# A two-layer decoder trunk on one core: casts set behind Pool's sums, zeros stored later, the join of the attention groups on Pool, fewer dense shares per strided item

## Chip, cores and metric

One core of one Trainium2 chip. The metric is device time in microseconds (us) of one execution; three runs of the kernel before gave 2818.04, 2818.78 and 2820.15, median 2818.78. Engines: PE = TensorE (matmuls), DVE = VectorE, ACT = ScalarE, POOL = GpSimd, SP = SyncE, which here issues all DMAs in one order. Each engine runs its instructions in the order of its own list.

## The reference, cut to what matters

Two layers over 1024 tokens of width 1024, in float32. Each layer adds to x the output of two attentions that run side by side, then that of a gated feed-forward part with a causal convolution.

```python
h = rmsnorm(x, norm1[l])
proj = h @ w_in[l]          # 1024 x 5120: q, k, v of both mixers, and the gates
o_a = dilated_mixture(qa, ka, va)        # 3 groups of 4 heads: dilation 1, 4, 16
o_b = stick_breaking_attention(qb, kb, vb)   # 4 heads
g_a, g_b = split(sigmoid(gate_pre + b_gate[l]))
x = x + (g_a * (o_a @ w_br[l, :256]) + g_b * (o_b @ w_br[l, 256:])) @ w_o[l]
h2 = rmsnorm(x, norm2[l])
a, v = split(h2 @ w_up[l])
x = x + (gelu(conv(a)) * v) @ w_down[l]
```

In the dilated mixture each group of heads does a softmax over a window of every 1st, 4th or 16th key, and the outputs of the three groups are added with weights proportional to their softmax denominators. The last step is a final RMSNorm.

## The kernel before

Every float32 operand of a large product is split into a high part (a cast to a rounded type on ACT, line 123) and a low part (source minus high part, on DVE, line 124); three matmuls of the parts make one product. Activations lie with features on the 128 partitions and tokens along the free axis, in two halves of 512 tokens. Part of the dense products are made with seven block products in place of eight (`pair`, `seven`): their operands are sums and differences of blocks of the weights (made in `pair`, lines 915 to 925) and of h (made in `block_sums`, lines 862 to 892: for the first two of four series Pool does three operations per sum, lines 871 to 873, into a buffer h_sum, and `split` casts it into t_hi and t_lo).

A layer's first part is a sequence of attention items, with dense products woven in. The items are 16 of the stick-breaking mixer (names B00 to B17), four of the group with dilation 1 (N00 to N11: scores z and lines 679 and 680, transposes t at line 688, parts p0h and p0l, products o at line 700), and 16 of the strided groups with dilation 4 and 16 (T00 to T17: scores z<-t_kq at lines 571 and 572, lines 780 and 781, transposes t at lines 786 to 788, parts p1h and p1l, products o at lines 796 and 798). Each item is cut into steps. After each step `Dense.advance(rate)` adds the item's rate to an account, and for every whole unit PE gets one share of dense work, six matmuls of 128x512 in `pair`. `RATE` holds the rates: stick-breaking, dilation 1, and the strided items of the first and of the second pair of heads. What dense work is left after the last item is done in `finish`. `Dense.aside`, called once per step, takes the next piece of side work from a list as soon as the item that it names is done; the 16 sums of h are that list. A strided item may begin when its keys and queries, fetched into t_kq, have had six shares of time. PE's order is the program's order; a scheduler orders the other engines and SP from estimated times.

`join(pr)` (lines 809 to 839) puts the groups together for a pair of heads, after the last strided item of that pair: small DVE steps on 128x16 tiles make the weights (lines 818 to 827), a DMA writes them to df, four DMAs bring them back broadcast over the partitions as fn and ft (line 833), and four DVE operations make `on` = `on` x fn + ot x ft (lines 834 to 839). After the second join, `in_two` in `mixer` casts `on` into oh_a and ol_a, and the branch product br_ps (lines 149 to 151) reads them, first for the first pair of heads and then for the second.

In layer 0, `mixer` also fills `none` with zeros on Pool (line 1069) and stores it four times into tk (line 1073), since the low part of the queries fills only half of its rows. `first` loads x in eight pieces xr and normalizes them with gb, a broadcast of the gains held in the buffer with the tag "ot".

Of the kernel before, what the change touches and what calls it, by code (L numbers as in the profile page):

```python
# [6 lines left out]
F32 = mybir.dt.float32  # L7
# [4 lines left out]
ALU = mybir.AluOpType  # L12
# [3 lines left out]
P = 128  # L16
# [21 lines left out]
IN_ORDER = {ET.PE, ET.Activation, ET.DVE, ET.Pool}  # L38
HEAD = 4
SECOND = 0.35  # L40
RATE = (0.68, 0.85, 1.0, 0.85)
PLAIN = 8
LEAD = 6
AHEAD = 200
# [2 lines left out]
def f32(ap):  # L47
    return ap.bitcast(F32)
# [3 lines left out]
def trunk_kernel(ctx, tc, x, norm1, w_in, b_gate, w_br, w_o, norm2, w_up, conv_w, conv_b, w_down, norm_f, out, depth=None, probe=None):  # L52
    nc = tc.nc
    act, dve, pe, pool = nc.scalar, nc.vector, nc.tensor, nc.gpsimd
# [4 lines left out]
    sb = ctx.enter_context(tc.tile_pool(name="sb", bufs=1))  # L59
# [45 lines left out]
    tk = [dr.tile([2, 4, P, 6, 256], F32, name=f"tk{i}") for i in range(2)]  # L105
# [16 lines left out]
    def split(hi, lo, src):  # L122
        act.copy(hi, src)  # L123
        dve.tensor_tensor(lo, src, f32(hi), ALU.subtract)  # L124
# [292 lines left out]
    S, B = {}, {}  # L417
# [392 lines left out]
    def join(pr):  # L810

        st, on, ot = R["st1", pr], R["on"], R["ot", pr]
        sn = sb.tile([P, 2, 2, 2, 4], F32, tag="sn", bufs=1, name="sn")
        nc.sync.dma_start(sn.rearrange("j a s n r -> j (a s) n r"), tok_view(dn[pr]))
        nat, far_ = (t.rearrange("j a s n r -> j a (s n r)") for t in (sn, st))
        w = sb.tile([P, 6, 16], F32, tag="sw", bufs=1, name="sw")
        f = sb.tile([P, 2, 16], F32, tag="sf", bufs=1, name="sf")
        dve.tensor_tensor(w[:, 0, :], nat[:, 0, :], far_[:, 0, :], ALU.min)
        dve.tensor_tensor(w[:, 1, :], w[:, 0, :], nat[:, 0, :], ALU.subtract)
        dve.tensor_tensor(w[:, 2, :], w[:, 0, :], far_[:, 0, :], ALU.subtract)  # L820
        act.activation(w[:, 1:3, :], w[:, 1:3, :], AF.Exp)
        dve.tensor_tensor(w[:, 3, :], w[:, 1, :], nat[:, 1, :], ALU.mult)
        dve.tensor_tensor(w[:, 4, :], w[:, 2, :], far_[:, 1, :], ALU.mult)
        dve.tensor_tensor(w[:, 3, :], w[:, 3, :], w[:, 4, :], ALU.add)
        dve.reciprocal(w[:, 5, :], w[:, 3, :])
        dve.tensor_tensor(f[:, 0, :], w[:, 1, :], w[:, 5, :], ALU.mult)
        dve.tensor_tensor(f[:, 1, :], w[:, 2, :], w[:, 5, :], ALU.mult)
        nc.sync.dma_start(tok_view(df[pr]), f.rearrange("j a (s n r) -> j (a s) n r", s=2, n=2))
        fn = sb.tile([P, T], F32, tag="p4", bufs=4, name="fn")
        ft = sb.tile([P, T], F32, tag="p4", bufs=4, name="ft")  # L830
        for a, t in enumerate((fn, ft)):
            for s in range(2):
                nc.sync.dma_start(t[64 * s : 64 * s + 64, :], df[pr][2 * a + s, :].partition_broadcast(64))
        dve.tensor_tensor(on[:, pr, :], on[:, pr, :], fn, ALU.mult)
        for n in range(2):
            src = ot.rearrange("p (r n j) -> p n j r", r=4, n=2)[:, n]
            fv = ft.rearrange("p (n j r) -> p n j r", n=2, r=4)[:, n]
            dve.tensor_tensor(fv, src, fv, ALU.mult)
        dve.tensor_tensor(on[:, pr, :], on[:, pr, :], ft, ALU.add)


    def half(n, k):
# [17 lines left out]
    def block_sums():  # L860


        keep = {}

        def first(t, a, b, i):
            if i == 0:
                if "r" not in keep:
                    keep["r"] = quarter("h_sum")
                new_s(t)
            r, (ah, al), (bh, bl) = keep["r"][:, i, :], a()[i], b()[i]  # L870
            pool.tensor_tensor(r, f32(al), f32(bl), ALU.subtract)
            pool.tensor_tensor(r, r, f32(ah), ALU.add)
            pool.tensor_tensor(r, r, f32(bh), ALU.subtract)
            split(*S[t][i], r)

        def further(t, a, i):
            if t == 4:

                S[4] = half(0, 0)
            elif i == 0:  # L880
                new_s(t)
            r, (ah, al) = keep["r"][:, i, :], a()[i]
            dve.tensor_tensor(r, f32(ah), r, ALU.subtract)
            dve.tensor_tensor(r, r, f32(al), ALU.add)
            split(*S[t][i], r)

        b11, b12, b21, b22 = (lambda n=n, k=k: half(n, k) for k in range(2) for n in (1, 0))
        todo = [({"B17"}, lambda i=i: first(3, b22, b12, i)) for i in range(4)]
        todo += [({"N01s"}, lambda i=i: first(1, b12, b11, i)) for i in range(4)]
        todo += [({"N11s"}, lambda i=i: further(2, b22, i)) for i in range(4)]  # L890
        todo += [({"plain"}, lambda i=i: further(4, b21, i)) for i in range(4)]
        return todo

    def pair(dense, l, offs, tiled, put):

# [168 lines left out]
    def mixer(l, pending):  # L1064
        R.clear()
        if l == 0:
            masks()
            none = sb.tile([P, 8, 256], F32, tag="xa", bufs=4, name="none")
            pool.memset(none[0:64], 0.0)
            for pr in range(2):  # L1070
                for g in range(2):
                    there = tk[pr][:, :, 64:128, 3 * g + 2, :].rearrange("s r p c -> p (s r) c")
                    nc.sync.dma_start(there, none[0:64])
        vectors = setup(l)
        next(vectors)
        first_units = relay(heads.pop(l)[0], primed=True) if l else relay(head(l))
# [3 lines left out]
        dense = Dense()  # L1080
        dense.plain = [gate(l, c) for c in range(PLAIN)]
        dense.seven = [pair_gate(dense, l, e) for e in range(PLAIN // 2, KD)]
        dense.side = block_sums()

        def kq(name, pr, after, off, scale):
            offk, offq = (OFF_KB, OFF_QB) if name == "b" else (OFF_KA, OFF_QA)
# [16 lines left out]
        for pr in range(2):  # L1103
            for i in range(8):
                needs = ["b1"] if pr else []
                items.append((f"B{pr}{i}", needs, [], RATE[0], lambda pr=pr, i=i: stick_item(pr, i // 4, i % 4)))
        for pr in range(2):
            for s in range(2):
                items.append((f"N{pr}{s}", [f"0{pr}"], ["v0"], RATE[1], lambda pr=pr, s=s: near_item(pr, s)))
        for pr in range(2):  # L1110
            share = {}
            for i in range(8):
                if i % 4 == 0:
                    share = {}
                items.append((f"T{pr}{i}", [f"F{8 * pr + i}"], [], RATE[2 + pr], lambda pr=pr, i=i, share=share: far_item(dense, pr, i // 4, i % 4, share)))
        attend(dense, items)
# [7 lines left out]
        def in_two():  # L1124
            for nm, src in (("b", R["ob"]), ("a", R["on"])):
                hi, lo = big("oh_" + nm, F32R), big("ol_" + nm, F32R)
                for n in range(2):
                    for c in range(2):
                        sl = slice(n * HF, (n + 1) * HF)
                        split(hi[:, c, sl], lo[:, c, sl], src[:, c, sl])  # L1130
                oh[nm] = (hi, lo)

        branches()
        todo = [(n, e0 + i) for e0 in range(0, KD, 2) for n in range(2) for i in range(2)]
# [567 lines left out]
    def first():  # L1702
        gb = sb.tile([P, T], F32, tag="ot", name="gb")
        warm = sb.tile([P, 8], F32, tag="ss", bufs=2, name="warm")
        act.activation(warm[:, 0:1], eps, AF.Sqrt)
        wp = bank("t", "warm")
        for _ in range(WARM):
            pe.matmul(wp[:, 0:P], ident, ident, start=True, stop=True)
        for n in range(2):
            new_h(n)  # L1710
            for c in range(4):
                t0 = n * HF + c * P
                xr = sb.tile([P, T], F32, tag="p4", bufs=4, name="xr")
                nc.sync.dma_start(xr, xin[t0 : t0 + P, :])
                if n == 0 and c == 0:
                    nc.sync.dma_start(gb, norm1[0].partition_broadcast(P))
                sq = sb.tile([P, T], F32, tag="ql", bufs=2, name="xsq")
                ss = sb.tile([P, 8], F32, tag="ss", bufs=2, name="ss")
                act.activation(sq, xr, AF.Square, accum_out=ss[:, 0:1])
                act.activation(ss[:, 1:2], ss[:, 0:1], AF.Sqrt, bias=eps[:, 0:1], scale=1.0 / D)  # L1720
                dve.reciprocal(ss[:, 2:3], ss[:, 1:2])
                for e0 in (0, 4):
                    hd = slice(e0 * P, (e0 + 4) * P)
                    dve.scalar_tensor_tensor(xr[:, hd], xr[:, hd], ss[:, 2:3], gb[:, hd], ALU.mult, ALU.mult)
                    tp = bank("s", "x_t")
                    for e in range(4):
                        pe.transpose(tp[:, e * P : (e + 1) * P], xr[:, (e0 + e) * P : (e0 + e + 1) * P], ident)
                    tv = tp.rearrange("p (e t) -> p e t", e=4)
                    hi, lo = (h[:, e0 : e0 + 4, c * P : (c + 1) * P] for h in H[n])
                    split(hi, lo, tv)  # L1730
                yield
# [46 lines left out]
```

## Time and profile before

| what | value |
|---|---|
| median of three runs | 2818.78 us |
| the profiled execution | 2819.48 us |
| its span from first to last instruction | 2817.7 us |
| mean granted PE clock | 0.983 |
| busy PE, DVE, ACT, POOL | 2692.9, 2001.3, 1354.3, 658.4 us |
| layer 0, layer 1: first score of a strided item | 444.1, 1833.2 us |
| the same: br_ps that waits for oh_a starts | 613.3, 2004.2 us |

The profile page has, for the whole span: busy time per engine; the span in 40 slices; DMA queues; the chain that ended last; the costliest groups of instructions. Further views give the waits (which engine and line waited for whom: total us, times, longest), busy time in chosen windows (length; busy us and instructions of PE, of PE's weight loads, of DVE, ACT and POOL; granted PE clock; DMA share; GB/s), and the instructions in order of time. Matmuls are pipelined, so one that takes 0.39 us follows its neighbour by about 0.23 us.

### The profile page before, as it was taken

How to read it: one execution, taken by the hardware profiler on the slowest of the kernel's cores; microseconds unless marked ns; L12 is line 12 of the kernel's file. 1: busy time of each engine (PE TensorE's matmuls, PEld its weight loads, DVE VectorE, ACT ScalarE, POOL GpSimd, SP SyncE). 2: the span in 40 equal slices, each digit the busy share in tenths (PEclk: the TensorE clock that was granted, in tenths of full speed). 3: DMA queues.
4: the chain of work that ended last, by engine and by line, in shares of the span. 5: the costliest groups of instructions: out<-in, count | busy, mean ns of one | idle time of the engine just before them, and what ended most of it. 6: DMA issues, size and time to landing. Idle time of an engine off the chain costs nothing. (4 is left out here: it accounts for less than half of the span.)

```text
span 2817.7 us, 36591 instructions
## 1 busy us (share of the span) xinstructions
PE 2692.9 (96%) x13066; PEld 2247.1 (80%) x13066; DVE 2001.3 (71%) x2968; ACT 1354.3 (48%) x2494; POOL 658.4 (23%) x469
## 2 busy tenths in 40 slices
PE   8998999989999999999999989999799999999999
PEld 7877888868878888878888778888588787877888
DVE  5775656666678888887657755465658788888865
ACT  4655545455445455422345555454545455544225
POOL 1004111102234343431120041210122433433200
PEclk9999999989999999999999999999899999999999
DMA  4011258654334434588401122775732444446963
GB/s 140 27 49 59 78 155 260 189 192 159 88 120 140 159 129 148 196 326 294 177 33 36 42 72 83 202 232 173 238 102 79 132 137 165 142 157 223 332 244 120
DMA packets 362242, 424.77 MB, mean 151 GB/s; under 512 B 25180, under 2 KB 289740, under 8 KB 360524
## 3 DMA queue, kind: packets, MB, share of 16 engines
q1 hardware_dynamic: 362060, 422.44, 45.6%
q8 instruction: 103, 1.69, 0.3%
q14 instruction: 79, 0.65, 0.1%
HBM read 282.78 MB, written 139.59 MB: 150 GB/s over the span
## 5 line engine op out<-in xcount | busy, mean ns | idle before, releaser
L124 DVE TENSOR_TENSOR w_lo<-up_a,w_hi 128x512 fp32r<-128x512 f32 x240 | 231.7, 966 | 37.9 <-ACT w_hi L123 37.9
L123 ACT CAST w_hi<-up_a 128x512 fp32r<-128x512 f32 x240 | 149.4, 623 | 173.2 <-PE u_b L855 38.5
L1534 DVE TENSOR_TENSOR x<-x,d_ps 128x512 f32<-128x512 f32 (+1 forms) x228 | 152.4, 672 | 80.9 <-PE d_ps L1528 80.0
L1271 POOL TENSOR_TENSOR cv<-cv 128x512 f32<-128x512 f32 x88 | 125.4, 1435 | 266.3 <-DVE g L124 130.2
L124 DVE TENSOR_TENSOR g<-cv,g 128x512 fp32r<-128x512 f32 x154 | 168.0, 1101 | 0.1
L124 DVE TENSOR_TENSOR w_lo<-w_raw,w_hi 128x512 fp32r<-128x512 f32 x152 | 113.6, 753 | 67.2 <-ACT w_hi L123 63.5
L123 ACT CAST w_hi<-w_raw 128x512 fp32r<-128x512 f32 x152 | 93.9, 620 | 120.1 <-PE o_ps L150 66.5
L854 PE MATMUL u_a<-hh,w_hi 128*128 128x512 f32 x320 | 127.6, 399 | 19.0 <-ACT g L123 14.3
L123 ACT CAST w_hi<-in_a 128x512 fp32r<-128x512 f32 x120 | 74.5, 620 | 146.9 <-PE i_a L855 61.0
L124 DVE TENSOR_TENSOR w_lo<-in_a,w_hi 128x512 fp32r<-128x512 f32 x120 | 87.8, 732 | 80.3 <-ACT w_hi L123 80.1
L1526 PE MATMUL d_ps<-gd_in,w_hi 128*128 128x512 f32 (+1 forms) x340 | 130.7, 384 | 5.8 <-ACT g L123 5.8
L1527 PE MATMUL d_ps<-gd_in,w_hi 128*128 128x512 f32 (+1 forms) x340 | 130.6, 384 | 0.0
L1528 PE MATMUL d_ps<-gd_in,w_lo 128*128 128x512 f32 (+1 forms) x340 | 130.5, 384 | 0.0
L856 PE MATMUL u_a<-hh,w_lo 128*128 128x512 f32 x320 | 126.3, 395 | 4.2 <-DVE w_lo L124 4.2
L123 ACT CAST g<-cv 128x512 fp32r<-128x512 f32 x154 | 93.5, 620 | 76.3 <-DVE g L124 41.0
L855 PE MATMUL u_a<-hl,w_hi 128*128 128x512 f32 x320 | 126.2, 394 | 0.0
L854 PE MATMUL u_a<-t_hi,w_hi 128*128 128x512 f32 x320 | 124.7, 390 | 0.4 <-ACT u L1407 0.4
L856 PE MATMUL u_a<-t_hi,w_lo 128*128 128x512 f32 x320 | 124.6, 390 | 0.0
L855 PE MATMUL u_a<-t_lo,w_hi 128*128 128x512 f32 x320 | 124.6, 390 | 0.0
L614 DVE TENSOR_TENSOR_SCAN stay<-stay,zero 128x128 f32<-128x128 f32 (+3 forms) x64 | 86.9, 1357 | 38.7 <-ACT stay L612 38.5
L1526 PE MATMUL d_ps<-gd_in,wd 128*128 128x512 f32 (+1 forms) x292 | 114.0, 390 | 0.0
L1528 PE MATMUL d_ps<-gd_in,wd 128*128 128x512 f32 (+1 forms) x292 | 112.9, 387 | 0.0
(397 smaller groups left out, 8630.5 us busy)
## 6 DMA issues: line engine op xcount, KB each, us to landing
gd<-g SPq DMA_DIRECT2D x154, 512.0 KB, 3.4
gd_in<-gd SPq DMA_DIRECT2D x154, 512.0 KB, 6.1
up_a<-in_w_up_dram SPq DMA_DIRECT2D x80, 512.0 KB, 4.5
t_kq<-tk SPq DMA_DIRECT2D x32, 768.0 KB, 5.1
wd_raw<-in_w_down_dram SPq DMA_DIRECT2D x22, 1024.0 KB, 6.9
w_raw<-in_w_in_dram SPq DMA_DIRECT2D x80, 256.0 KB, 3.0
in_a<-in_w_in_dram SPq DMA_DIRECT2D x40, 512.0 KB, 5.4
gin<-gs SPq DMA_DIRECT2D x32, 512.0 KB, 4.3
```

The costliest lines, as they stand in the source:

```text
L123: act.copy(hi, src)
L124: dve.tensor_tensor(lo, src, f32(hi), ALU.subtract)
L614: dve.tensor_tensor_scan(rev, rev, zero[:, 0:1].to_broadcast([P, L]), 1.0, ALU.mult, ALU.add)
L854: pe.matmul(o, w[0][:, c], rh, start=(first and i == 0), stop=False, skip_group_check=True)
L855: pe.matmul(o, w[0][:, c], rl, start=False, stop=False, skip_group_check=True)
L856: pe.matmul(o, w[1][:, c], rh, start=False, stop=(last and i == 3), skip_group_check=True)
L1271: return lambda: pool.tensor_tensor(dst, a, dst, ALU.subtract)
L1526: pe.matmul(o[:, sub], wh[:, c], gh[:, sub], start=(i == 0 and k in (0, 4, 5)), stop=False, skip_group_check=True)
L1527: pe.matmul(o[:, sub], wh[:, c], gl[:, sub], start=False, stop=False, skip_group_check=True)
L1528: pe.matmul(o[:, sub], wl[:, c], gh[:, sub], start=False, stop=(i == m - 1), skip_group_check=True)
L1534: dve.tensor_tensor(x, x, o[:, sub], ALU.add)
```

## The change

There are four edits. `RATE` for the strided items falls from 1.0 and 0.85 to 0.72 and 0.62. The four operations at the end of `join` move from DVE to Pool. In `block_sums` the sum and its split become two pieces of side work: in the two series that Pool computes, the sums are begun every third step and each split follows four steps after its sum; in the two that DVE computes, the split follows one step later. The zeros are no longer filled and stored at the start, but as a piece of side work after item B02, from a buffer of half the size (in "ot") with eight stores instead of four.

```diff
-RATE = (0.68, 0.85, 1.0, 0.85)
+RATE = (0.68, 0.85, 0.72, 0.62)
...
-        dve.tensor_tensor(on[:, pr, :], on[:, pr, :], fn, ALU.mult)
+        pool.tensor_tensor(on[:, pr, :], on[:, pr, :], fn, ALU.mult)
...
-            dve.tensor_tensor(fv, src, fv, ALU.mult)
-        dve.tensor_tensor(on[:, pr, :], on[:, pr, :], ft, ALU.add)
+            pool.tensor_tensor(fv, src, fv, ALU.mult)
+        pool.tensor_tensor(on[:, pr, :], on[:, pr, :], ft, ALU.add)
...
             pool.tensor_tensor(r, r, f32(bh), ALU.subtract)
-            split(*S[t][i], r)
...
             dve.tensor_tensor(r, r, f32(al), ALU.add)
-            split(*S[t][i], r)
+
+        def in_two(t, i):
+            split(*S[t][i], keep["r"][:, i, :])
...
-        todo = [({"B17"}, lambda i=i: first(3, b22, b12, i)) for i in range(4)]
-        todo += [({"N01s"}, lambda i=i: first(1, b12, b11, i)) for i in range(4)]
-        todo += [({"N11s"}, lambda i=i: further(2, b22, i)) for i in range(4)]
-        todo += [({"plain"}, lambda i=i: further(4, b21, i)) for i in range(4)]
+        todo = []
+
+        def series(after, t, f, lag, gap):
+
+            at = {}
+            for i in range(4):
+                at.setdefault(i * gap, []).append(lambda i=i: f(i))
+                at.setdefault(i * gap + lag, []).append(lambda i=i: in_two(t, i))
+            for k in range(3 * gap + lag + 1):
+                todo.append((after, lambda fs=at.get(k, ()): [g() for g in fs]))
+
+        series({"B17"}, 3, lambda i: first(3, b22, b12, i), 4, 3)
+        series({"N01s"}, 1, lambda i: first(1, b12, b11, i), 4, 3)
+        series({"N11s"}, 2, lambda i: further(2, b22, i), 1, 1)
+        series({"plain"}, 4, lambda i: further(4, b21, i), 1, 1)
         return todo
+
+    def zeros():
+
+        none = sb.tile([P, 4, 256], F32, tag="ot", name="none")
+        pool.memset(none[0:64], 0.0)
+        for pr in range(2):
+            for g in range(2):
+                for s in range(2):
+                    nc.sync.dma_start(tk[pr][s, :, 64:128, 3 * g + 2, :].rearrange("r p c -> p r c"), none[0:64])
...
-            none = sb.tile([P, 8, 256], F32, tag="xa", bufs=4, name="none")
-            pool.memset(none[0:64], 0.0)
-            for pr in range(2):
-                for g in range(2):
-                    there = tk[pr][:, :, 64:128, 3 * g + 2, :].rearrange("s r p c -> p (s r) c")
-                    nc.sync.dma_start(there, none[0:64])
...
-        dense.side = block_sums()
+        dense.side = [({"B02"}, zeros)] * (l == 0) + block_sums()
```

## Prediction, on record before the changed kernel's time was known

> **What bounds the kernel now.** I read part 1 of the page first, then the waits of TensorE (PE), then the granted clock in windows around the longest of them, then the timeline there.
>
> ```profile
> PE 2692.9 (96%) x13066; PEld 2247.1 (80%) x13066; DVE 2001.3 (71%) x2968; ACT 1354.3 (48%) x2494; POOL 658.4 (23%) x469
> ```
>
> PE is the bound, and the change neither adds nor removes a matmul. Only its 2817.7 - 2692.9 = 124.8 us of idle time, and matmuls that ran at half clock, can be won. The waits of PE name whom it waited for (total us, times, longest):
>
> ```profile
> PE br_ps L149 <- ACT oh_a L123: 19.7, 2, 11.2
> PE o L700 <- ACT p0h L123: 18.5, 4, 6.4
> ...
> PE sb_t L625 <- DVE beta L615: 12.5, 10, 2.4
> PE z L571 <- DVE st L780: 8.5, 6, 2.1
> ...
> PE v_ps L149 <- ACT w_hi L123: 4.7, 1, 4.7
> ```
>
> Four of these lie where the change works: the join of the groups (oh_a), the casts around the sums of h (p0h), the scores during the first join (z), the start (v_ps). The windows show the second price, the seventh figure (PEclk) falling to 0.50 after idle:
>
> ```profile
> 258.70:269.00 10.30, 6.21 (x18) 5.05 (x19) 5.56 (x11) 5.57 (x16) 10.30 (x9) 0.50 0.31 120
> ...
> 279.20:282.60 3.40, 3.40 (x11) 2.71 (x11) 3.40 (x9) 2.70 (x7) 0.00 (x0) 0.50 0.44 128
> ...
> 535.20:542.00 6.80, 5.44 (x18) 4.57 (x19) 4.62 (x9) 4.19 (x11) 0.73 (x1) 0.50 0.35 117
> 589.80:593.20 3.40, 2.32 (x16) 2.03 (x17) 1.96 (x7) 1.39 (x4) 0.00 (x0) 1.00 0.51 131
> 593.20:596.60 3.40, 3.39 (x14) 2.71 (x14) 2.21 (x9) 2.79 (x9) 0.00 (x0) 0.50 0.65 275
> ```
>
> A half-clock window costs half of PE's busy time in it: 3.1 us in the first.
>
> **1. Start (layer 0 only).** SP issues four 512 KB stores of zeros at 7.2 us, ahead of the third and fourth w_raw loads; these land at 22.3 and 23.0, and PE idles 4.67 us until 23.0. In the changed order the fourth xr and the two w_raw stand there, behind only the DVE splits of the first two w_raw, which ended at 9.9 and 11.6; with some 4 us to landing the weights are there by 16, while PE has work until 18.3. The gap goes, and the 3.2 us after it at 0.21 us per matmul (0.12 from 26.3 on) shrink to about half. I take 6 us; the ends are 0 (another load binds) and 8. The zeros, now eight stores of 256 KB, stand behind the last xr and wait for the last reader of gb, since they share its buffer; SP had nothing to issue from 31.6 to 51.2, and 2 MB at 150 to 250 GB/s take 8 to 14 us, so they hide there. Without that cover the next w_raw would be up to 10 us late.
>
> **2. Casts of the sums.** The timeline shows the chain (start, length, last what ended the idle time):
>
> ```profile
> 254.75 1.73 POOL L871 TENSOR_TENSOR h_sum<-hl 128x512 f32<-128x512 f32 x1
> ...
> 255.26 1.77 DVE L124 TENSOR_TENSOR w_lo<-w_raw,w_hi 128x512 fp32r<-128x512 f32 x1
> ...
> 260.62 0.62 ACT L123 CAST t_hi<-h_sum 128x512 fp32r<-128x512 f32 x1 [5.88 <-POOL h_sum L873]
> ...
> 262.65 0.58 PE L700 MATMUL o<-p0h,v 128*128 128x256 f32 x1 [6.42 <-ACT p0h L123]
> ```
>
> ACT is in order: the cast of the third sum waits 5.88 us for Pool, the cast of p0h stands behind it, and PE waits. Layer 0 pays 6.42 + 2.91 + 0.62 idle and 3.1 + 1.7 at half clock, 14.7 us; layer 1 (1648 to 1683) 14.6. In the changed order p0h stands ahead, and the four casts of the first series stand together after the copies of the second half of the keys. Counted in shares (six matmuls at 0.227, 1.36 us) ACT gets there at about 261.7, when the twelve Pool operations from 245.1 are done (261.8). The next p0h is then ready at 265.5, just when PE wants it, its low part at 266.1. The second series starts on Pool when the first cast has freed h_sum (264), takes 12 x 1.28 = 15.4 us, and ends at 279.5 to 280.5; PE wants the p0h behind it at 281.9. So nothing long is left, but two places with no margin: I leave 1.4 us of stalls per layer and take 13.2 x 2 = 26.4 us. Ends: 18 (each place costs 2 us and a half-clock window) and 29.
>
> **3. The strided stage and its end.** From the first z<-t_kq to the br_ps that waits for oh_a took 444.1 to 613.3 = 169.2 us, in layer 1 1833.2 to 2004.2 = 171.0. The instruction orders hold 75 dense shares there before and after. Two items with twelve shares took 21.65 us (446.4 to 468.1), so an item's own work is (21.65 - 12 x 1.36) / 2 = 2.65 and PE's work is 16 x 2.65 + 75 x 1.36 = 144.4 us. The rest is waiting and half clock. Before, no share was left for the last two items; now ten shares and four pairs of transposes and products, 16.6 us, stand after the last score.
>
> What ends last is the chain of the join:
>
> ```profile
> 606.83 1.22 DVE L834 TENSOR_TENSOR on<-on,fn 128x1024 f32<-128x1024 f32 x1 [2.28 <-DMA fn<-df]
> ...
> 609.35 1.98 DVE L838 TENSOR_TENSOR ft<-ot,ft 128x512 f32<-128x512 f32 x2 [1.30 <-DMA ft<-df]
> ...
> 611.37 1.22 DVE L839 TENSOR_TENSOR on<-on,ft 128x1024 f32<-128x1024 f32 x1
> ...
> 612.63 1.14 ACT L123 CAST oh_a<-on 128x512 fp32r<-128x512 f32 x2 [1.55 <-DVE on L839]
> ```
>
> Scores (594.1), small DVE steps (to 598.4), df out and fn, ft back (609.3), three multiplies and adds, cast, PE: 19.2 us from last score to br_ps, 21.4 in layer 1. The change lengthens it twice. On Pool a 128x512 operation takes 1.28 (the h_sum rows), so 128x1024 some 2.5: after ft two of 1.28 and one of 2.5 stand for 1.98 + 1.22, +1.9 us (the multiply by fn hides between the landings of fn and ft). Strided Pool operations are in no row; the dearest simple one took 3.1 (L915), hence +0 to +5.5. And a w_lo that waits for PE to free a buffer (3.4 us after the last score) now stands before the last small steps: +2.6. The chain becomes 23.7 and 25.8 us.
>
> Then layer 0 needs 144.4 - 16.6 + 23.7 = 151.5 plus stalls s, layer 1 153.6 + s: they save 17.7 - s and 17.4 - s.
>
> s: fewer shares mean less time for DVE and ACT. Between a pair of transposes and the product that reads it lay 3.0 to 4.7 us; now about nine of 32 have 1.6. The chain needs 0.05 + 0.47 + 0.05 + 0.56 = 1.15, with one foreign cast (0.62) before it 1.75. I put 2.5 us on these, 0.9 on two scores that now stand together (as at 592.4), and 2.5 on the first join: Pool's 8 us of work meet DVE's splits, and the w_lo above took 1.77 against 0.69 alone because a Pool sum ran. Behind that split p1l and the scores wait. On the other side the DVE join at 529 to 537, which cost 3.4 us of idle and 2.7 at half clock, is gone. One half-clock window, 1.7, comes on top; rounded, s = 8, ends 3 and 14. So 9.5 per layer, 19 us; ends 7 and 29.
>
> The Trainium skill, page "SBUF — State Buffer", section "SBUF: two separate sides", says that Pool and a DVE operation with two SBUF inputs lock a shared port for the whole instruction, the other blocking. The trace agrees (1.77 against 0.69); by it a split beside the 2.5 us multiply can wait all of it, four such locks per first join.
>
> **Sum**, against the profiled execution's 2819.48 us (span 2817.7; the median of the runs, 2818.78, is 0.7 below): 2819.5 - 6 - 26.4 - 19 = **2768 us**.
>
> **Rivals.**
> (a) Short stalls bring no half clock, queues stay short, s = 3: 2768 - 10 = 2758. For it: twenty-odd gaps of 0.84 to 1.5 us had 1.00 after them. Against: the window 589.8 to 593.2, 2.32 of 3.40 busy, was followed by 0.50. The page "TensorE: Matmul & The Clock Gate" of the Trainium skill, section "What's actually happening", has the half rate come after an idle window of some 3.4 us, which would favour this rival; the trace differs, since that window held no such gap.
> (b) The end of the join eats its gain: strided Pool operations at 3.1, gate loads late behind the last stores: +5 to +8 per layer, 2768 + 13 = 2781.
> (c) The casts still wait: Pool's sums late by 3 us each and a half-clock window every time, 6 us per layer: 2780.
> (d) Slower: the thin cover makes the strided stage a chain of half-clock windows. A missed cover costs about 1.1 us and then 1.7; the 51 us are gone at 18 misses, 9 of 16 items in each layer. For it: 1.6 us of cover. Against: covers of 1.8 and 2.1 us at 540 to 580 showed no gap. At 24 misses: 2768 + 67 = 2835.
> (e) The orders move and nothing else, PE waits elsewhere: 2819.
>
> **Chances.** Forecast (2762 to 2775) 0.45; (a) 0.20; (b) 0.13; (c) 0.10; two of (b), (c) and a start without gain together, 2790 to 2800, 0.05; (d) 0.05; (e) 0.02. The range 2750 to 2796 leaves out (d), (e), and gains at every upper end. Faster by over 0.2% (about what a measurement of this kernel can tell from no change) 0.93, within 0.02, slower 0.05.
>
> **What would show it.** Right: v_ps without a 4.7 us gap before 25 us; no L700 wait over 1 us; the oh_a wait down from 8.5 and 11.2 to some 5 to 7 although its chain is longer; z waits under 1.5 us; a few L796 waits of 0.2 to 1 us. Wrong, if p0h still waits for the sums, if PEclk is below 0.9 in several slices of the strided stage, or if the keys' weights at 50 us come late behind the zeros.

## The result, and the profile after

The changed kernel takes 2775.99 us (median of four runs, 2774.71 to 2777.19). The kernel before, run beside it, takes 2819.47 (2818.04 to 2821.08). The ratio is 0.9846, 95% interval 0.9829 to 0.9863: faster by 1.5%. The forecast was 2768; 51.4 us were to be saved, 43.5 are (44.6 between the two profiled spans, 2817.7 and 2773.1).

Part 1 of the page of the changed kernel (busy us, share of the span, instructions):

```profile
PE 2679.4 (97%) x13066; PEld 2237.9 (81%) x13066; DVE 1989.5 (72%) x2952; ACT 1354.6 (49%) x2494; POOL 691.9 (25%) x485
```

PE has the same 13066 instructions. Its idle time fell from 124.8 to 93.7 us (span less busy), and its busy time by 13.5 us. Some 10 us of that are half clock: PE was busy for 58.8 us at half clock before and for 39.1 after, and half of such time is lost. DVE gave 16 instructions to Pool. The waits of PE in the changed kernel (total us, times, longest):

```profile
PE br_ps L149 <- ACT oh_a L123: 15.6, 2, 9.4
...
PE br_ps L149 <- ACT br_w L123: 7.8, 2, 6.7
...
PE o L700 <- DVE p0l L124: 4.5, 2, 2.3
...
PE o L796 <- DVE p1l L124: 3.6, 7, 0.8
...
PE z L571 <- DVE st L780: 1.4, 2, 0.7
...
PE o L700 <- ACT p0h L123: 0.5, 2, 0.3
```

The wait for p0h, 18.5 us before, is 0.5. The wait of the scores z is 1.4 for 8.5. The 4.7 us of v_ps at the start are gone. Two rows grew by over 2 us: p0l (1.2 us before) and br_w (5.3 us before in three waits, now with one of 6.7).

A table by stretches shows where the time went. Each is read from the starts of the named instructions on PE, in both profiled executions:

| stretch | before, layers 0 and 1 | after | saved | forecast |
|---|---|---|---|---|
| start to first score z of layer 0 | 77.1 | 69.0 | 8.1 | 6 |
| first score to first strided score | 367.0, 367.7 | 357.8, 358.1 | 18.7 | 26.4 |
| first strided score to the br_ps that waits for oh_a | 169.2, 170.9 | 156.4, 158.3 | 25.4 | 19 |
| from there to the first product u_ps | 141.6, 140.5 | 143.8, 144.6 | -6.3 | 0 |
| all the rest | | | -1.4 | 0 |

The sum is 44.6 before rounding. Against the forecast two terms gave more (+2.1, +6.4), one less (-7.7), and 7.6 us were lost where it had put nothing.

### The profile page after: what moved, and what is told of

It reads as the page before. It is cut to its first block, busy times and chain, and to the rows that moved or that the text cites. A ratio compares the mean times of both kernels' runs of the same rounds, so it can differ in the third digit from the quotient of the medians.

```text
span 2773.1 us, 36571 instructions
## 1 busy us (share of the span) xinstructions
PE 2679.4 (97%) x13066; PEld 2237.9 (81%) x13066; DVE 1989.5 (72%) x2952; ACT 1354.6 (49%) x2494; POOL 691.9 (25%) x485
## 5 line engine op out<-in xcount | busy, mean ns | idle before, releaser
L123 ACT CAST g<-cv 128x512 fp32r<-128x512 f32 x154 | 93.6, 620 | 77.1 <-DVE g L124 41.4
```

## The experiments

In the first four kernels one of the four edits is undone.

**The rates.**

```diff
-RATE = (0.68, 0.85, 0.72, 0.62)
+RATE = (0.68, 0.85, 1.0, 0.85)
```

> The changed kernel with the old rates 1.0 and 0.85, the other three edits kept. Theory (the ten shares left for the end fill the chain of the join, 24.4 and 27.5 us from last score to the branch product): without them the wait for oh_a grows from 6.2 and 9.4 us by the 16.6 us of work that stood there, less some 3 us per layer of short waits that the emptier queues cost; time about 2776 + 2 x 13 = 2802 us (2797 to 2808). Rival (most of the 12.7 us that each strided stage won is the first join leaving DVE, 3.4 us idle and 2.7 at half clock): only the other half comes back, about 2776 + 2 x 6.5 = 2789 us.

Measured: 2792.0 us (2787.9 to 2796.3), ratio to the kernel before 0.9904 (0.9889 to 0.9919). From the first strided score to the waiting br_ps it takes 169.2 and 172.1 us, 12.7 and 13.8 more than in the changed kernel. That is the theory's size, stretch by stretch, and the rival's half is not seen there. It does not come as the theory had it, all through the wait for oh_a, which is 10.2 and 12.8 us, 4.0 and 3.4 more: the last score comes 15.8 and 17.2 us later in the stage, and from its end to the waiting br_ps it takes 21.0 and 23.8 us, 3.0 and 3.5 less, with little work and much half clock in it.

The time as a whole misses the theory's range and lies nearer to the rival's 2789. It rises by 16 us by the medians and by 21 between the profiled executions (the one profiled here is the slowest of its four). With the old rates the stretch behind the join is 1.3 and 3.6 us shorter, which accounts for the 21; the reason comes with the kernel for the branch weights. With the old rates and the join on Pool the strided stretch is about as long as it was before the change (169.2, 170.9): without shares behind the last score, the join on Pool brings nothing.

**The join.** The four operations go back to DVE.

```diff
-        pool.tensor_tensor(on[:, pr, :], on[:, pr, :], fn, ALU.mult)
+        dve.tensor_tensor(on[:, pr, :], on[:, pr, :], fn, ALU.mult)
...
```

> The changed kernel with the four operations of both joins back on DVE. Theory (Pool helps at the first join and hurts at the last): the last join ends 3.2 us earlier per layer (1.22 + 1.98 + 1.22 for 2.34 + 2.98 + 2.34 us), the wait for oh_a falls from 6.2 and 9.4 to about 3 and 6 us; the first join stalls PE again by up to 3.4 us idle and 2.7 at half clock per layer; 2776 - 6.5 + 12 = 2782 us. Rival (with fewer dense shares beside it DVE takes the first join without a stall of PE): 2776 - 6.5, and up to 4 less where the branch weights of layer 1 come earlier: 2765 to 2770 us.

Measured: 2780.88 us (2777.34 to 2781.85), ratio 0.9862 (0.9848 to 0.9877), 5 to 6 us above the changed kernel: the theory's side. The timeline of this kernel at the first join, DVE and then PE (start, length, last in brackets what ended the idle time):

```profile
500.15 1.23 DVE L834 TENSOR_TENSOR on<-on,fn 128x1024 f32<-128x1024 f32 x1 [3.37 <-DMA fn<-df]
...
505.42 1.22 DVE L839 TENSOR_TENSOR on<-on,ft 128x1024 f32<-128x1024 f32 x1
506.55 0.42 DVE L780 CUSTOM_DVE_ANT_1 p<-z,bias 128x256 f32<-128x256 f32 x1
```

```profile
507.03 0.48 PE L571 MATMUL z<-t_kq 128*128 128x128 f32 x1 [4.56 <-DVE st L780]
```

DVE stands for 3.37 us at an operation that waits for a DMA, and the step of the next scores (L780) stands behind the join. PE had done the scores that this step reads by 502.5. From 500.15 on DVE works without a pause: 4.42 us of the join and 2.06 of other operations come before L780. An estimate from these rows: without the join's 4.42 us L780 would come at 502.1, and with a join that began 3.37 us earlier at 503.2; in the changed kernel it comes at 502.8. So neither the wait nor the length costs much alone; what hurts is a long piece of work that can't begin before its data lands, in the list ahead of a step that PE needs. On Pool nothing that is needed soon stands there; the changed kernel's wait at this place is 0.75 us. At the last join it is the other way round: with DVE the wait for oh_a is 4.8 and 5.9 us instead of 6.2 and 9.4. The lines of the last join in the changed kernel, layer 0, Pool:

```profile
574.64 2.40 POOL L834 TENSOR_TENSOR on<-on,fn 128x1024 f32<-128x1024 f32 x1 [24.54 <-DMA fn<-df]
577.17 2.98 POOL L838 TENSOR_TENSOR ft<-ot,ft 128x512 f32<-128x512 f32 x2
580.23 2.34 POOL L839 TENSOR_TENSOR on<-on,ft 128x1024 f32<-128x1024 f32 x1
```

A 128x1024 operation takes 2.34 to 2.40 us for 1.22 on DVE, a strided one of 128x512 takes 1.49 for 0.99; together 7.7 for 4.4, and cast and branch product wait for the end of it.

**The casts.** `block_sums` as before, each split behind its sum.

```diff
             pool.tensor_tensor(r, r, f32(bh), ALU.subtract)
+            split(*S[t][i], r)
...
-        series({"B17"}, 3, lambda i: first(3, b22, b12, i), 4, 3)
+        todo = [({"B17"}, lambda i=i: first(3, b22, b12, i)) for i in range(4)]
...
```

> The changed kernel with the sums of h as before, each cast right behind its sum. Theory (the trace of the changed kernel shows 9.1 and 9.6 us won between the first score of a layer and the first of its strided stage): the L700 waits of 6.4 and 2.9 us are back in both layers, about 2776 + 19 = 2795 us. Rival (the 26.4 us of the prediction, a part of it spent on half-clock windows elsewhere that are not due to this edit): 2800 to 2803 us.

Measured: 2795.13 us (2792.73 to 2801.0), ratio 0.9912 (0.9896 to 0.9929): the theory's 19 us, below the rival's 2800. The L700 waits for p0h are back with 6.44 and 4.10 us in layer 0 and 6.40 and 3.08 in layer 1.

**The zeros.** Filled and stored at the start, as before.

```diff
+            none = sb.tile([P, 8, 256], F32, tag="xa", bufs=4, name="none")
+            pool.memset(none[0:64], 0.0)
...
-        dense.side = [({"B02"}, zeros)] * (l == 0) + block_sums()
+        dense.side = block_sums()
```

> The changed kernel with the zeros filled and stored at the start as before. Theory (first score of layer 0 at 69.0 for 77.1 us, all of it due to the zeros): about 2776 + 8 = 2784 us, with the 4.7 us wait of v_ps back. Rival (only the gap itself counts, the half clock until 16.7 or 26.6 us is the chip's start and the same in both): 2776 + 4.7 = 2781 us.

Measured: 2777.16 us (2776.44 to 2781.8), ratio 0.9855 (0.984 to 0.987). The trace says the theory (first score at 77.1, v_ps wait 4.97), the median does not: it lies 1.2 and 2.4 us above the two medians of the changed kernel (the second is shown further on), less than theory or rival had (8 and 4.7). The execution profiled is the slowest of the four. This was tried again below.

Next, the two rows of the wait table that were not foreseen, and the last join.

**Last join on DVE, first on Pool.**

```diff
-        pool.tensor_tensor(on[:, pr, :], on[:, pr, :], fn, ALU.mult)
+        (dve if pr else pool).tensor_tensor(on[:, pr, :], on[:, pr, :], fn, ALU.mult)
...
```

> The changed kernel with the first join of a layer on Pool and the last one on DVE. Theory (Pool helps where the join lies beside scores and hurts where it is the chain's end): the first join keeps its short wait of 0.7 us, the last one ends 3.2 us earlier, the wait for oh_a falls from 6.2 and 9.4 to about 3 and 6 us; 2776 - 6.5 = 2769.5 us (2766 to 2772). Rival (what the last join gains is lost right behind it, to the branch weights and gates that then come late, as in the run with both joins on DVE, 1962.8 to 2104.7 us in layer 1 against 1953.3 to 2097.9): 2774 to 2777 us.

Measured: 2768.98 us (2765.99 to 2771.59), ratio 0.9816 (0.9798 to 0.9833), against 2774.72 of the changed kernel on the same chip: the theory's size. The waits for oh_a are 4.74 and 6.31 us.

**The branch weights.** In the changed kernel, layer 1, ACT and PE:

```profile
1966.32 0.62 ACT L1170 CAST hh<-mrg 128x512 fp32r<-128x512 f32 x1 [1.95 <-DVE mrg L1206]
1966.84 1.13 ACT L123 CAST w_hi<-w_raw 128x512 fp32r<-128x512 f32 x2
...
1972.65 1.33 ACT L123 CAST br_w<-br_raw 128x512 fp32r<-128x512 f32 x2 [2.21 <-DMA br_raw<-in_w_br_dram]
```

```profile
1973.32 0.80 PE L149 MATMUL br_ps<-oh_a,br_w 128*128 128x512 f32 x1 [6.73 <-ACT br_w L123]
```

The loads of br_raw were issued at 1968.86, once the splits of w_raw, which uses the same buffers, were through; and those splits stood on ACT behind the third cast of hh. With the old rates, and before the change, ACT's order in layer 1 was one cast of hh, one of w_raw, one of hh; with the new rates the scheduler put three casts of hh first, with the join on either engine. So this wait belongs to the edit of the rates. The kernel that tests it moves the load of w_raw:

```diff
-        next(wo[0])
         next(residual, None)
         for i, (n, e) in enumerate(todo):
+            if i == 4: next(wo[0])
```

> The changed kernel with the first load of the output weights (w_raw of w_o) moved behind four outputs of the branch product. Theory (the second set of branch weights is late because its buffers are held by that w_raw, whose cast stands on ACT behind the third cast of hh): the wait of br_ps for br_w falls from 6.7 us in layer 1 and 1.0 in layer 0 to under 1.5 in both, and the half clock after it goes; 2776 - 6 = 2770 us. Rival (they are late because SP stands at a load of gin ahead of them): the waits stay, 2776 us, or later output weights make it 2778.

Measured: 2770.68 us (2764.12 to 2771.33), ratio 0.9813 (0.9796 to 0.983). The 6.73 us wait is 0.94, and 1.46 at the next set; from the waiting br_ps of layer 1 to u_ps it takes 140.6 us instead of 144.6. The theory holds.

**The changed kernel again**, unchanged, on the chip of these four.

> The changed kernel itself on this chip, for comparison: 2774 to 2778 us. The half-clock windows lie on a grid of 3.41 us that is placed anew in each execution, so the times of one kernel should differ by one or two windows, 1.7 us each.

Measured: 2774.72 us (2773.02 to 2777.31), ratio 0.9834 (0.9819 to 0.9848).

**Pool's second series cut short.**

```diff
-            pool.tensor_tensor(r, r, f32(ah), ALU.add)
-            pool.tensor_tensor(r, r, f32(bh), ALU.subtract)
+            if t == 3: pool.tensor_tensor(r, r, f32(ah), ALU.add)
+            if t == 3: pool.tensor_tensor(r, r, f32(bh), ALU.subtract)
```

> The changed kernel in which Pool leaves out two of three operations of the second series of sums (lines 872 and 873 there), so that its output is not the reference's; Pool is then idle at 262 to 265 us. Theory (the 2.25 us wait of o<-p0l at 265 and 1634 us comes from Pool's sums, which stretch the DVE split w_lo ahead of p0l from 0.69 to 1.75 us and the operation ahead of that): w_lo takes 0.69 us, the wait falls to 1 us or less, and no half-clock window follows it. Rival (DVE's order alone, two foreign operations ahead of p0l): the wait stays over 1.8 us. In the time, theory: some 5 us less than the changed kernel's; rival: the same.

The kernel leaves out two of Pool's three operations per sum of that series, so only its waits say something, not its result. Measured: one run of 2769.25 us. First the timeline of the changed kernel, Pool and DVE, then the same three DVE operations in this one:

```profile
261.69 1.28 POOL L872 TENSOR_TENSOR h_sum<-h_sum,hh 128x512 f32<-128x512 f32 x1
261.89 1.23 DVE L665 TENSOR_SCALAR bias<-base 128x256 f32<-128x256 bf16 x1
...
262.93 1.31 POOL L871 TENSOR_TENSOR h_sum<-hl,hl 128x512 f32<-128x512 f32 x1
263.04 1.75 DVE L124 TENSOR_TENSOR w_lo<-w_raw,w_hi 128x512 fp32r<-128x512 f32 x1
...
264.71 0.68 DVE L124 TENSOR_TENSOR p0l<-t,p0h 128x512 fp32r<-128x512 f32 x1
```

```profile
262.77 0.29 DVE L665 TENSOR_SCALAR bias<-base 128x256 f32<-128x256 bf16 x1
262.98 0.68 DVE L124 TENSOR_TENSOR w_lo<-w_raw,w_hi 128x512 fp32r<-128x512 f32 x1
263.67 0.69 DVE L124 TENSOR_TENSOR p0l<-t,p0h 128x512 fp32r<-128x512 f32 x1
```

From the first of the two operations ahead of p0l to p0l itself it takes 0.90 us here, where Pool is done at 262.9, and 2.82 beside its sums. PE's wait for p0l falls from 2.25 to 0.34 us in both layers, no half-clock window follows it, and the stretch from the first score to the first strided score is 3.4 and 3.3 us shorter. The theory holds: it was Pool's sums, not DVE's order. The page "SBUF — State Buffer" of the Trainium skill, section "SBUF: two separate sides", names DVE operations with two SBUF inputs or in a two-port mode as those that lock out Pool or are locked out by it; these rows agree for w_lo. L665, which has one input, is stretched as well (0.29 to 1.23); whether it runs in such a mode no run here shows.

**Both edits together.**

```diff
+        (dve if pr else pool).tensor_tensor(on[:, pr, :], on[:, pr, :], fn, ALU.mult)
...
+            if i == 4: next(wo[0])
```

> The changed kernel with the last join on DVE and the first load of the output weights moved behind four branch outputs. Theory (two separate waits at the end of the stage, oh_a and br_w): the gains add, 2775 - 5.7 - 4 = 2765 us (2762 to 2768). Rival (both edits take the same time out, since the branch product waits for whatever is late next): 2769 us, that of the better one alone.

Measured: 2761.94 us (2760.82 to 2762.2), ratio 0.98 (0.9784 to 0.9816). The gains add, as the theory had it (2765), and 3 us more came, of which the cause is not shown.

**The zeros, a second time**, undone in that kernel with the diff shown above.

> The kernel before in this list, with the zeros filled and stored at the start as before. Theory (first score of layer 0 at 77.1 instead of 69.0 us in the traces): 8 us more than its neighbour without this edit, 2773 us. Rival (the median of the run with the zeros undone, 2777.2 against 2776.0 and 2774.7, was only 1 to 2 us above the changed kernel, so the start costs less outside the profile, or the time comes back later): 2766 to 2767 us.

Measured: 2766.96 us (2766.24 to 2771.86), ratio 0.9822 (0.9805 to 0.984), 5.0 us above its neighbour, between the two. The first score is at 76.3 for 68.9 us, so the start loses 7.4; of this 1.4 us come back up to the first strided score, where the half-clock window that its neighbour has at 184.2 us has no counterpart, and 1.8 up to u_ps. The zeros are worth 5 us here and 1 to 2 by the medians of the first try; their worth isn't settled more closely than that.

**More work behind the last score.**

```diff
-RATE = (0.68, 0.85, 0.72, 0.62)
+RATE = (0.68, 0.85, 0.66, 0.55)
...
-LEAD = 6
+LEAD = 5
```

> The kernel with both edits, with rates of 0.66 and 0.55 and a strided item allowed five shares after its fetch instead of six, so that 25.7 us of PE's work stand after the last score instead of 16.3. Theory (what counts is how much work stands there, up to the length of the chain, some 21 and 24 us with the last join on DVE): the waits for oh_a of about 4.7 and 6.3 us and the half clock after them, two windows or 3.4 us per layer, go, about 2765 - 16 = 2749 us, of which short waits in the stage may take 2 to 6: 2749 to 2756. Rival (the thinner cover costs what the end gains, as the forecast's slower case had it: scores late, waits over 1.85 us within a window and half clock after them): 2765 us or more.

Measured: 2755.37 us (2751.78 to 2757.57), ratio 0.9775 (0.9758 to 0.9792), 6.6 us below the kernel with both edits, the fastest here, inside the theory's range, but not by its mechanism. The waits for oh_a are gone, yet one of their length stands in each layer at another place. Waits of PE, and then DVE and PE in layer 0 of this kernel:

```profile
PE i_b L854 <- DVE u L966: 12.2, 2, 6.3
```

```profile
561.78 1.23 DVE L834 TENSOR_TENSOR on<-on,fn 128x1024 f32<-128x1024 f32 x1 [3.28 <-DMA fn<-df]
...
573.45 0.69 DVE L966 TENSOR_TENSOR u<-u,i_c 128x512 f32<-128x512 f32 x1
```

```profile
574.20 0.79 PE L854 MATMUL i_b<-hh,w_hi 128*128 128x512 f32 x1 [5.94 <-DVE u L966]
```

DVE, which has the last join here, waits for fn and ft and then does the splits of oh_a; L966, for whose result a dense share waits, stands behind all that. What was won lies elsewhere, in part in the waits for the branch weights, 2.7 us in layer 1 of the kernel with both edits and none here, and in the short waits for p1l, which don't occur here. The last join on Pool together with this cover, which should free DVE for L966, wasn't tried. Rate and lead were changed together, so what each is worth isn't shown. The rival's thin cover is not seen: the longest wait for a score in the strided stage is 0.64 us.

**The casts later.**

```diff
-        series({"B17"}, 3, lambda i: first(3, b22, b12, i), 4, 3)
+        series({"B17"}, 3, lambda i: first(3, b22, b12, i), 7, 3)
```

> The kernel with both edits, where each cast of the first series follows seven steps after its sum instead of four, so that the second series, which needs the same buffer, runs later on Pool. Theory (the wait of o<-p0l, 2.25 us and a half-clock window per layer, is Pool's second series meeting DVE's split): the second series no longer runs at 262 to 265 us, the wait falls under 1 us, 2765 - 6 = 2759 us. Rival (the collision moves to the next split in a chain of PE's, or p0h waits for the late casts): 2764 to 2770 us.

Measured: 2762.67 us (2758.62 to 2763.7), ratio 0.98 (0.9783 to 0.9818); the wait for p0l is 2.26 and 2.24 us as ever. This tells nothing of the theory: the instructions of every engine came out in the same order as without the edit, and Pool's second series ran at the same place relative to DVE's split. Three steps of program order moved nothing in the scheduler's lists, so this is in effect a second measurement of the kernel with both edits, 0.7 us from the first.

## Why the prediction was right, step by step

**Direction and order of size** held: every one of the four edits wins something beside the other three, PE stays the bound, and nothing turned slower. The time lies in the range, 8 us above the forecast.

**Start, 6 forecast, 8.1 in the trace, 1 to 5 by the runs.** w_raw was issued at 9.9 and 10.7 us instead of 13.5 and 15.8, the gap is gone, and PE's matmuls go at the full rate from 16.7 us on instead of 26.6. The zeros go out from 32.1 to 45.0 us, in the stretch that was named, and no wait of PE follows.

**Casts, 26.4 forecast, 18.7 measured.** The mechanism held: p0h is 0.3 us late instead of 6.4. What failed is "its low part at 266.1", 0.6 us behind p0h: it came 2.6 us behind, because Pool's second series stretched the two DVE operations ahead of it. That is 2.25 us and a half-clock window per layer (4.2 us with the 0.3 of p0h, against the 1.4 put there); the prediction had the lock for the joins, with the 1.77 us row in its hand, and did not apply it to the sums that it had itself moved to this place. Two more windows, at 184.0 and 1552.7 us, follow a wait of 2.43 us for beta that the kernel before had as well, but without half clock; why is told below.

**Strided stage, 19 forecast, 25.4 measured.** The arithmetic of the stage held: 10 shares stand behind the last score, and the chain from there takes 24.1 and 27.3 us (forecast 23.7 and 25.8). The term that was mis-sized is s, 8 us: 156.4 - (144.4 - 16.6 + 24.1) = 4.5 in layer 0, 158.3 - (127.8 + 27.3) = 3.2 in layer 1. Of that only 2.8 and 2.4 us are idle time of PE ahead of the last score; the rest is work that the sum had too small. Rival (a) with s = 3 was near on this point. The short waits for p1l are 0.2 to 0.8 us, and no half-clock window lies between 270 and 579 us. The first join on Pool costs 0.75 and 0.69 us, not 2.5.

**Behind the join, 0 forecast, -6.3 measured.** The sum ended at the br_ps that waits for oh_a. Rival (b) named gate loads late there; it was branch weights, at half of its price (4.1 us in layer 1; in layer 0 1.3 of 2.2 us are such waits, the rest is not explained). What failed is the nothing that the sum put there: a lower rate also changes what the scheduler does after the stage, and ACT's order there was not read.

**Rival (d)** did not come near: with s at 3 to 5 us the cover was far from the point at which it decides, and with the still thinner cover of more_cover PE idles 1.6 us per layer ahead of the last score, less than in the changed kernel.

**Luck in the number.** The terms of the sum were off by up to 7.7 us each, in both directions, and their errors cancel to 6.8; that 2776 lies within 8 us of the forecast owes something to this.

The edits do not add up one by one. From the first strided score to u_ps, both layers together, the kernel before takes 622.2 us; with the rates alone (undo_join, beside casts and zeros) 608.9, with Pool alone (undo_rate) 624.6, with both 603.1. Pool alone loses 2.5 us and beside the rates wins 5.8.

## What to carry to other kernels

Work moved to a slow engine pays where the operation waits for a DMA and a busy engine's list, with a step that is needed soon in it, would stand behind it, and costs where the operation is itself the end of a chain; so decide it for each place, not for the line of code. When work is put beside a chain, look at what else runs then on the engine that shares a port with it: the moved sums doubled the DVE split that PE waited for. Carry the sum past the wait that you remove to the next stage, and read the order of the engines there too.

## What the runs showed of the hardware

The half clock of PE goes by windows of 3.41 us on a grid that lies differently in each execution (its first border, divided by 3.413 us, left a remainder of 0.06 to 3.30 in the 14 traces), and by how much PE idles within one window. Two windows of the changed kernel, each with the one behind it (length; busy us and count of PE, PE's weight loads, DVE, ACT, POOL; granted clock; DMA share; GB/s):

```profile
180.59:184.00 3.41, 0.98 (x8) 0.75 (x7) 3.41 (x4) 1.78 (x3) 0.00 (x0) 1.00 0.03 10
184.00:187.41 3.41, 3.41 (x13) 2.84 (x12) 2.39 (x6) 1.55 (x4) 0.00 (x0) 0.50 0.00 0
502.46:505.87 3.41, 2.66 (x16) 2.24 (x16) 2.46 (x9) 2.51 (x8) 3.22 (x3) 1.00 0.70 218
505.87:509.29 3.42, 3.42 (x22) 2.94 (x21) 1.52 (x3) 2.27 (x6) 2.39 (x1) 1.00 0.70 241
```

The first has 2.43 us of idle time (the wait for beta), and half clock follows; the second has 0.75 (the wait for a score), and full clock stays.

In the kernel before the same wait for beta, 2.43 us, fell across a border of the grid, and full clock followed:

```profile
187.03:190.44 3.41, 2.42 (x15) 1.93 (x13) 2.49 (x2) 3.37 (x7) 0.00 (x0) 1.00 0.26 79
190.44:193.86 3.42, 1.98 (x11) 1.72 (x12) 3.36 (x6) 1.31 (x5) 0.00 (x0) 1.00 0.00 0
193.86:197.27 3.41, 3.41 (x21) 2.94 (x20) 2.46 (x7) 1.88 (x5) 0.00 (x0) 1.00 0.25 73
```

Over all windows of the 14 traces that had full clock: with 2.0 us idle or more, half clock followed in 140 of 140; with 1.84 to 2.0 in 13 of 16; with 1.2 to 1.84 in 4 of 115; with 0.8 to 1.2 in 3 of 285 (one of them the window at 589.8 of the kernel before, which the prediction leaned on). At half clock, 0.6 us of idle were enough to stay there, in 70 of 70. (A grid laid slightly differently shifts these counts by one or two.) So at full clock a wait under 1.8 us that is alone in its window mostly cost only itself here; a longer one cost up to 1.7 us more for each window that then ran at half clock, or nothing more, by where it fell, which may be part of the 1 to 10 us by which the runs of one kernel differ. The page "TensorE: Matmul & The Clock Gate" of the Trainium skill, section "What's actually happening", has a free-running window of 3413 ns and half rate after an idle one; the traces agree on the window, and show that some 2 us of idle time in it are enough. In the kernel before, half clock is recorded for 96.6 us in all, in the changed one for 55.0.
